# Attention of a decoder trunk: the last rotation two steps behind the last projection, and the last head's output normed and split by halves

## The chip, the cores and the metric

The kernel runs on one core of a Trainium2 chip. The metric is the device time of one launch in microseconds (us), as the median of three runs. Five engines work beside each other: TensorE (PE, with its weight loads PEld), VectorE (DVE), ScalarE (ACT), GpSimd (POOL) and SyncE (SP), which only issues DMAs here.

## The reference, cut to what matters

Two layers over 1024 positions of width 1024, in float32: gated linear attention with its MLP, then differential attention with its MLP. The change lies in the second layer's attention:

```python
k, v = shared_kv(h, kv_norm_w, w_kv, cos, sin)     # projections, rotary on k
q = apply_rope((a_in @ w_q), cos, sin)             # 8 heads, two q and two k of width 64 each
p = softmax(where(causal, q @ k.T * scale, -inf))  # per head and pair
a = p[:, 0] - lam * p[:, 1]                        # the differential weights
o = rmsnorm(a @ v, subln_w) * (1 - lam_init)       # per head, width 128
h = h + o.reshape(S, 1024) @ w_o
```

Rotary is x * cos + rot(x) * sin, where rot swaps the two halves of a head and negates one.

## The kernel before

Every float32 product is made of three products of a rounded high part and a rest: hi x hi, hi x lo, lo x hi (names ending in h and l: xh and xl, wh and wl, ah and al). The high part is an ACT copy, the low part a DVE or POOL subtraction (helper `lo_of`, line 115, or `tt`, line 112).

The attention is one loop over steps s = -2, -1, ... for 8 heads of 8 query blocks (64 blocks in all). Step s issues, in this order: the scores of block s+2 (sp); the values of a pair of blocks if s-1 is odd (pv: the weighted sum of v, then ACT copies osq and osb out of it); `turn(s)` (PE transposes the weights e into tp, ACT copies them to ah, DVE makes al); `combine(s+1)` (DVE makes e from two exponentials); `weights(s+2)` (DVE takes the row maximum mx, ACT the exponential e); splits of the next head's q, k and v; then the step's fill units; and the norm of the head that ended: `squares` and `norm1` at s-2 (DVE rs_m, POOL's power rs_y), `norm2` at s-3 (DVE rs_t, ro) and `finish` at s-4 (PE spreads ro over rows into rb, DVE multiplies osb by it).

Fill units keep PE busy between these. `spread(units, s0, s1)` spreads a list evenly over steps s0 to s1. There are 48 projection half-units (`rope_unit`, twelve matmuls into pf each) for the q and k of heads 2 to 7. Four make one q or k: the second part of each half ends in an ACT copy xsb and a DVE product y with the cosines; after the second half SP issues four DMAs that put xsb's halves in swapped places (xw). At the start of the next unit `rope_end` lets POOL multiply xw by the sines and add it to y, and a later unit stores y to DRAM (kd, qd), from where it is loaded as st and split. Only the last rotation is called on its own, on DVE (RE). A weight tile is fetched with `take`: ACT makes wh, DVE wl, and DVE multiplies the next raw tile by the norm's gains.

The outputs of heads 0 to 5 are stored (osp) and loaded again (osr, `o_load`), then split by an ACT copy xh and eight POOL subtractions for two tiles (`o_split`). Sixteen units of the output projection (`wo_unit`, into dwo) for heads 0 to 3 fill the last steps; those of heads 4 to 7 follow the loop, and six of them begin inside it with three of their four parts (heads 4 to 6), so that only the last head is missing.

PE, ACT and SP go in written order (`manual_schedule`); the order of DVE and POOL is set by a scheduler at build time. PSUM has two double-bank tiles for scores and output products and four single banks for all else (pf, tp, pv, rb, sv).

Of the kernel before, what the change touches and what calls it, by code (L numbers as in the profile page):

```python
# [10 lines left out]
F32R = mybir.dt.float32r  # L11
BF16 = mybir.dt.bfloat16
AF = mybir.ActivationFunctionType
ALU = mybir.AluOpType
# [6 lines left out]
NB = S // P  # L21
# [4 lines left out]
AH, HD, VD = 8, 64, 128  # L26
# [4 lines left out]
DORD = (0, 4, 1, 5, 2, 6, 3, 7)  # L31
# [17 lines left out]
def trunk(  # L49
# [26 lines left out]
    PE, ACT, DVE, POOL = nc.tensor, nc.scalar, nc.vector, nc.gpsimd  # L76
# [10 lines left out]
    def uid(s):  # L87
        count[0] += 1
        return f"{s}_{count[0]}"

    def U(name, dt=F32):
        return up.tile([P, 1026], dt, tag="u", name=uid(name))[:, 0:1024]
# [4 lines left out]
    def PS(name):  # L97
        return pp.tile([P, 512], F32, tag="p", name=uid(name))

    def PS2(name):  # L100
        return pp.tile([P, 1024], F32, tag="p2", name=uid(name), bufs=2)
# [6 lines left out]
    def H(hf):  # L108
        return slice(hf * HALF, (hf + 1) * HALF)

    def tt(eng, o, a, b, op):
        eng.tensor_tensor(out=o, in0=a, in1=b, op=op)  # L112

    def stt(eng, o, a, s, b, op0, op1):
        eng.scalar_tensor_tensor(out=o, in0=a, scalar=s, in1=b, op0=op0, op1=op1)  # L115

    def lo_of(eng, lo, x, hi, scale=1.0):
        stt(eng, lo, x, scale, hi.bitcast(F32), ALU.mult, ALU.subtract)
# [144 lines left out]
    def take():  # L263
        prefetch(1)
        r = ready.popleft()
        prefetch(AHEAD)
        return r
# [37 lines left out]
    def bcast_rows(col8, sl):  # L305

        ps = PS("rb")
        for i, b in enumerate(range(sl.start // P, sl.stop // P)):
            PE.matmul(ps[:, i * P:(i + 1) * P], col8[:, b:b + 1].broadcast_to([P, P]), ident, start=True, stop=True)  # L309
        return ps  # L310

    def fine(eng, o, a, b, op):

        for c in range(0, 1024, 256 if eng is POOL else 1024):
            q = slice(c, c + 256 if eng is POOL else 1024)
            tt(eng, o[:, q], a[:, q], b[:, q], op)

    def split(x, scale=1.0, eng=DVE):
        xh = U("xh", F32R)
        xl = U("xl", F32R)  # L320
        ACT.activation(xh, x, AF.Copy, scale=scale)
        if eng is POOL:
            fine(POOL, xl, x, xh.bitcast(F32), ALU.subtract)
        else:
            lo_of(DVE, xl, x, xh, scale)
        return xh, xl
# [92 lines left out]
    class Late:  # L419
# [44 lines left out]
        def spread(self, sl):  # L464
            ps = bcast_rows(self.rtok, sl)[:, 0:sl.stop - sl.start]
            if self.g is None:
                DVE.tensor_copy(self.rbc[:, sl], ps)
                return
            ACT.activation(self.rbc[:, sl], ps, AF.Copy)
            for q in range(0, sl.stop - sl.start, 256):  # L470
                self.ps[sl.start + q] = ps[:, q:q + 256]
# [713 lines left out]
    sub_w = const.tile([P, 1], F32, name="sub_w")  # L1185
# [85 lines left out]
    def kq_units(hh):  # L1271
        return [(rope_unit, dst, sc, hf, part) for dst, sc in ((kd[hh], 1.0), (qd[hh], HD ** -0.5))
                for hf in range(2) for part in range(2)]

    class Attn:
# [130 lines left out]
        def finish(self):  # L1406
            for hf in range(2):
                stt(DVE, self.osb[:, H(hf)], self.osb[:, H(hf)], sub_w, bcast_rows(self.ro, H(hf)), ALU.mult, ALU.mult)

    osp = [dram.tile([P, S], F32, name=f"osp{i}") for i in range(AH - 2)]  # L1410
    h, on, wdo = {}, [], {}
    n1 = Wide(G_FFN1, hs[1])
# [15 lines left out]
    def o_split():  # L1428
        on.append(split(osr.popleft(), eng=OE))

    def wo_unit(g, d, hf, ks=range(4)):

        e, j = divmod(d, 4)
        if (g, j) not in wdo:
            wdo[g, j] = take() + ([None] * 4,)
            if g == 1 and j < 2:
                t = PS2("dwo")
                wdo[g, j][2][0], wdo[g, j][2][2] = t[:, H(0)], t[:, H(1)]
        wh, wl, ops = wdo[g, j]
        u = e * 2 + hf  # L1440
        if ops[u] is None:
            ops[u] = PS("dwo")
        o = ops[u]
        sl = H(hf)
        for k in ks:
            wd = slice(k * 2 * P + e * P, k * 2 * P + e * P + P)
            a, b = on[4 * g + k]
            PE.matmul(o, wh[:, wd], a[:, sl], start=(k == 0), stop=False)  # L1448
            PE.matmul(o, wl[:, wd], a[:, sl], start=False, stop=False)  # L1449
            PE.matmul(o, wh[:, wd], b[:, sl], start=False, stop=(k == 3))  # L1450
        if 3 not in ks:
            return
        ops[u] = None
        tt(DVE, h[d][:, sl], o, h[d][:, sl], ALU.add)
        if g == 1:
            n1.add(d, hf, h[d])
        if hf == 1:
            if e == 1:
                del wdo[g, j]
            if d == ND - 1:  # L1460
                on[4 * g:4 * g + 4] = [None] * 4

    steps = AH * NB
    OE = POOL
    KQE, OL, OS, RS, WOB, RE = 46, 45, 46, 47, 48, DVE
    AHEAD, LOADS = 1, 2
    heads = {0: Attn(0)}
    todo = {0: [(heads[0].load, 2)], 6: [(heads[0].load, 1)], 9: [(heads[0].qk_split, 1), (heads[0].v_split,)],
# [9 lines left out]
    fill = {s: [] for s in range(-2, steps)}  # L1478
# [4 lines left out]
            fill[s0 + s] += units[len(units) * s // n:len(units) * (s + 1) // n]  # L1483

    spread([u for a in range(2, AH) for u in kq_units(a)], -2, KQE)
    fill[KQE + 1].append((rope_end, RE))
    fill[KQE + 1].append((rope_end,))
    spread([(o_load, q) for q in range(4)], OL, OL + 1)
    spread([(o_split,) for q in range(4)], OS, OS + 1)
    fill[RS] += [(residual, d) for d in DORD]  # L1490
    spread([(o_load, q) for q in (4, 5)], steps - 4, steps - 3)
    spread([(wo_unit, 0, d, hf) for d in DORD for hf in range(2)], WOB, steps - 1)

    for s in range(-2, steps + 5):
        a, i = divmod(s + 2, NB)
        if a < AH:
            hd = heads[a]
            if i == 0:
                hd.begin()
            hd.scores(i)  # L1500
        b, j = divmod(s - 1, NB)
        if 0 <= s - 1 < steps and j % 2 == 1:
            heads[b].values(j // 2)
        b, j = divmod(s, NB)
        if 0 <= s < steps:
            heads[b].turn(j)
        if 0 <= s + 1 < steps:
            b, j = divmod(s + 1, NB)
            heads[b].combine(j)
            if j % 2 == 0:  # L1510
                heads[b].clear(j // 2)
        if a < AH:
            hd.weights(i)
            if i == 1 and a > 0:
                hd.v_split()
            if a + 1 < AH:
                if i == 2:
                    heads[a + 1] = Attn(a + 1)
                    heads[a + 1].load(1)
                if i == 4:  # L1520
                    heads[a + 1].load(0)
                    heads[a + 1].qk_split(1)
                if i == 6:
                    heads[a + 1].qk_split(0)
                    heads[a + 1].load(2)
        for f, *args in fill.pop(s, ()):
            f(*args)
        if 0 <= s - 2 < steps:
            b, j = divmod(s - 2, NB)
            if j % 2 == 1:  # L1530
                heads[b].squares(j // 2)
            if j == NB - 1:
                heads[b].norm1()
        if 0 <= s - 3 < steps:
            b, j = divmod(s - 3, NB)
            if j == NB - 1:
                heads[b].norm2()
        if 0 <= s - 4 < steps:
            b, j = divmod(s - 4, NB)
            if j == NB - 1:  # L1540
                hd = heads.pop(b)
                hd.finish()
                if b < AH - 2:
                    nc.sync.dma_start(osp[b], hd.osb)
                elif b == AH - 2:
                    last = [split(hd.osb, eng=POOL)]
                else:
                    last.append(split(hd.osb))
        if s == steps - 1:
            AHEAD, LOADS, WENG = 1, 3, DVE  # L1550
            o_split()
            o_split()
            on.append(last[0])
        if steps <= s < steps + 3:
            for d in DORD[2 * (s - steps):2 * (s - steps) + 2]:
                wo_unit(1, d, 0, range(3))
    on.append(last[1])
    for hf in range(2):
        for u, d in enumerate(DORD):
# [110 lines left out]
```

## Time and profile before

| | before |
|---|---|
| median of three runs | 2395.2 us (2393.8 to 2397.9) |
| profiled execution | 2395.9 us, of which the span 2393.9 us |
| PE busy | 2320.7 us, 97% of the span |
| DVE, ACT, POOL busy | 77%, 43%, 30% |
| attention loop | about 1251 to 1667 us |

The profile follows one execution; busy time is that of instructions, and the idle time of an engine is put down to what released it. [...]

### The profile page before, as it was taken

What the parts mean: (1) busy time and instruction counts of PE and PEld (TensorE: products, weight loads), DVE (VectorE), ACT (ScalarE), POOL (GpSimd) and SP (SyncE); (2) the same over time, 40 slices, a digit from 0 to 9 for tenths busy, and PEclk for the clock granted to TensorE, in tenths of its full rate; (3) what the DMA queues carried; (4) which work ended last, traced back from release to release, by engine and by line L of the source; (5) the groups of instructions that cost most, each with busy time, mean ns of one, the idle gap of its engine ahead of it and who ended that gap; (6) DMA issues with size and microseconds to landing.
All of it is one profiled execution on the core that took longest, in us unless ns stands there. A gap on an engine that the chain in (4) does not pass through costs nothing. (4 is left out here: it accounts for less than half of the span.)

```text
span 2393.9 us, 29738 instructions
## 1 busy us (share of the span) xinstructions
PE 2320.7 (97%) x10926; PEld 1878.5 (78%) x10926; DVE 1832.5 (77%) x2599; ACT 1040.5 (43%) x1864; POOL 729.8 (30%) x725
## 2 busy tenths in 40 slices
PE   8999999999999999999999999999999999999998
PEld 6878877767888888888877888777767888888886
DVE  7454454699999999867138787666799999999875
ACT  4533442354333434544125555544344443334553
POOL 3211101045544431000005564623036554441001
PEclk9999999999999999999999999999899999999999
DMA  5012124113323248424243333522213333238433
GB/s 184 1 53 71 36 98 171 61 52 116 115 84 115 84 165 304 133 85 171 79 128 118 113 123 93 163 107 84 84 35 117 113 100 115 84 126 317 142 92 101
DMA packets 101425, 271.22 MB, mean 113 GB/s; under 512 B 10272, under 2 KB 23200, under 8 KB 101280
## 3 DMA queue, kind: packets, MB, share of 16 engines
q1 hardware_dynamic: 101280, 269.34, 32.8%
q8 instruction: 85, 1.39, 0.2%
q14 instruction: 60, 0.49, 0.1%
HBM read 184.89 MB, written 76.02 MB: 109 GB/s over the span
## 5 line engine op out<-in xcount | busy, mean ns | idle before, releaser
L899 PE MATMUL pf<-xp,wp 128*128 128x512 f32 x1232 | 488.5, 397 | 12.8 <-DVE wp L115 12.7
L900 PE MATMUL pf<-xp,wp 128*128 128x512 f32 x1232 | 488.0, 396 | 1.8 <-DVE xp L115 1.4
L898 PE MATMUL pf<-xp,wp 128*128 128x512 f32 x1232 | 487.8, 396 | 1.5 <-ACT xp L206 1.2
L899 PEld LDWEIGHTS pf<-xp,wp 128*128 128x128 f32 x1232 | 232.2, 188 | 73.4 <-DVE wp L115 19.5
L898 PEld LDWEIGHTS pf<-xp,wp 128*128 128x128 f32 x1232 | 232.2, 189 | 58.9 <-ACT xp L206 3.2
L900 PEld LDWEIGHTS pf<-xp,wp 128*128 128x128 f32 x1232 | 232.0, 188 | 58.8 <-DVE xp L115 5.4
L1007 PE MATMUL out<-rp,lp 128*128 128x512 f32 (+1 forms) x632 | 246.4, 390 | 0.6 <-ACT rp L206 0.6
L1009 PE MATMUL out<-rp,lp 128*128 128x512 f32 (+1 forms) x632 | 246.1, 389 | 0.0
L115 DVE SCALAR_TENSOR_TENSOR c<-u,cv,c 128x1024 f32<-128x1024 f32 x176 | 245.9, 1399 | 0.0
L1008 PE MATMUL out<-rp,lp 128*128 128x512 f32 (+1 forms) x632 | 245.5, 388 | 0.0
L115 DVE SCALAR_TENSOR_TENSOR wp<-raw,wp 128x512 fp32r<-128x512 f32 x180 | 202.5, 1134 | 13.2 <-ACT wp L206 12.9
L112 DVE TENSOR_TENSOR u<-pf,u 128x512 f32<-128x512 f32 x300 | 200.6, 681 | 15.0 <-PE pf L900 10.0
L276 PE MATMUL pf<-xh,wh 128*128 128x512 f32 x458 | 187.4, 409 | 8.9 <-ACT wh L196 8.9
L277 PE MATMUL pf<-xh,wl 128*128 128x512 f32 x458 | 181.6, 396 | 1.8 <-DVE wl L115 1.8
L278 PE MATMUL pf<-xl,wh 128*128 128x512 f32 x458 | 181.1, 395 | 0.0
L112 POOL TENSOR_TENSOR rs_y<-rs_m,nhalf 128x4 f32<-128x4 f32 (+2 forms) x26 | 31.4, 1206 | 481.8 <-DVE rs_m L292 451.1
L925 ACT ACTIVATE c<-c 128x1024 f32<-128x1024 f32 x44 | 46.7, 1062 | 267.0 <-DVE c L115 267.0
L115 DVE SCALAR_TENSOR_TENSOR wp<-wt,wp 128x512 fp32r<-128x512 f32 x128 | 151.6, 1186 | 2.5 <-ACT wp L206 2.5
L1007 PEld LDWEIGHTS out<-rp,lp 128*128 128x128 f32 x632 | 118.7, 188 | 27.5 <-ACT rp L206 1.1
L1009 PEld LDWEIGHTS out<-rp,lp 128*128 128x128 f32 x632 | 118.7, 188 | 27.6 <-DVE rp L115 0.8
L1008 PEld LDWEIGHTS out<-rp,lp 128*128 128x128 f32 x632 | 118.8, 188 | 26.8
L112 POOL TENSOR_TENSOR wt<-raw,wt 128x512 f32<-128x512 f32 x40 | 56.9, 1423 | 253.9 <-DVE wp L115 253.9
(250 smaller groups left out, 4997.8 us busy)
## 6 DMA issues: line engine op xcount, KB each, us to landing
raw<-in_w_in SPq DMA_DIRECT2D x88, 512.0 KB, 3.8
tr<-td SPq DMA_DIRECT2D x70, 512.0 KB, 4.0
td<-c SPq DMA_DIRECT2D x44, 512.0 KB, 2.8
wo<-in_w_out SPq DMA_DIRECT2D x44, 512.0 KB, 8.4
raw<-in_w_gla SPq DMA_DIRECT2D x24, 512.0 KB, 5.9
h<-hs SPq DMA_DIRECT2D x24, 512.0 KB, 4.9
td<-mt SPq DMA_DIRECT2D x22, 512.0 KB, 3.8
hs<-h SPq DMA_DIRECT2D x32, 256.0 KB, 2.0
```

The source lines that it names most:

```text
L112: eng.tensor_tensor(out=o, in0=a, in1=b, op=op)
L115: eng.scalar_tensor_tensor(out=o, in0=a, scalar=s, in1=b, op0=op0, op1=op1)
L276: PE.matmul(o, wh[:, k], xh[:, H(hf)], start=(k == 0), stop=False)
L277: PE.matmul(o, wl[:, k], xh[:, H(hf)], start=False, stop=False)
L278: PE.matmul(o, wh[:, k], xl[:, H(hf)], start=False, stop=(k == ND - 1))
L898: PE.matmul(o, wh, xh, start=(k == 0), stop=False)
L899: PE.matmul(o, wl, xh, start=False, stop=False)
L900: PE.matmul(o, wh, xl, start=False, stop=(k == ND // 2 - 1))
L925: ACT.activation(gt, gt, AF.Silu)
L1007: PE.matmul(o, wh, xh, start=(j == 0 or cut and j == NJ - LASTF), stop=False)
L1008: PE.matmul(o, wl, xh, start=False, stop=False)
L1009: PE.matmul(o, wh, xl, start=False, stop=(j == NJ - 1 or cut and j == NJ - LASTF - 1))
```

## The change

Six constants and the end of the loop are changed. KQE, the last step with a projection unit, goes from 46 to 45, so each unit of all heads comes one step sooner, the first at step -2. The last rotation stays at step 47 and its store moves to step 48. The loads of the first four heads' outputs go from steps 45 and 46 to 44 and 45 (OL), their splits from 46 and 47 to 44 and 45, into the same step as the load (OS). The residual loads go from step 47 to 46 (RS). The output units' first step goes from 48 to 47 (WOB); 16 units over 17 steps leave the first of them empty, so they stay where they are. For the last head, `finish` and the split of a whole tile, which came after all six three-part output products, become `finish_split` between the fifth and the sixth, half by half.

```diff
+        def finish_split(self):
+            xh, xl = U("xh", F32R), U("xl", F32R)
+            for hf in range(2):
+                o = self.osb[:, H(hf)]
+                stt(DVE, o, o, sub_w, bcast_rows(self.ro, H(hf)), ALU.mult, ALU.mult)
+                ACT.activation(xh[:, H(hf)], o, AF.Copy)
+                lo_of(DVE, xl[:, H(hf)], o, xh[:, H(hf)])
+            return xh, xl
...
-    KQE, OL, OS, RS, WOB, RE = 46, 45, 46, 47, 48, DVE
+    KQE, OL, OS, RS, WOB, RE = 45, 44, 44, 46, 47, DVE
...
-    fill[KQE + 1].append((rope_end, RE))
-    fill[KQE + 1].append((rope_end,))
+    fill[KQE + 2].append((rope_end, RE))
+    fill[KQE + 3].append((rope_end,))
...
-    for s in range(-2, steps + 5):
+    for s in range(-2, steps + 3):
...
-            if j == NB - 1:
+            if j == NB - 1 and b < AH - 1:
...
-                elif b == AH - 2:
+                else:
                     last = [split(hd.osb, eng=POOL)]
-                else:
-                    last.append(split(hd.osb))
...
-            for d in DORD[2 * (s - steps):2 * (s - steps) + 2]:
-                wo_unit(1, d, 0, range(3))
+            for u in range(2 * (s - steps), 2 * (s - steps) + 2):
+                if u == 5:
+                    last.append(heads.pop(AH - 1).finish_split())
+                wo_unit(1, DORD[u], 0, range(3))
```

The scheduler's order on DVE follows. First DVE in a regular head, from the 768-wide maxima (mx) or just behind them to the 896-wide ones; wl is a weight tile's low part and raw the next tile times the gains. Before:

```order
L115 SCALAR_TENSOR_TENSOR e_12011<-e_12012,rc_12107,e_12011 128x768
L115 SCALAR_TENSOR_TENSOR wl_12026<-raw_11763,wh_12025 128x1024
L115 SCALAR_TENSOR_TENSOR osb_11058<-osb_11058,sub_w,rb_12051 128x512
L115 SCALAR_TENSOR_TENSOR osb_11058<-osb_11058,sub_w,rb_12057 128x512
L1340 TENSOR_REDUCE mx_12111<-sp_12064 128x1
L1340 TENSOR_REDUCE mx_12111<-sp_12065 128x1
L112 TENSOR_TENSOR raw_12030<-raw_12030,gains_sb 128x1024
```

And now:

```order
L115 SCALAR_TENSOR_TENSOR wl_11981<-raw_11720,wh_11980 128x1024
L1340 TENSOR_REDUCE mx_12040<-sp_12007 128x1
L115 SCALAR_TENSOR_TENSOR al_11883<-tp_12023,ah_11882 128x4x128
L1340 TENSOR_REDUCE mx_12040<-sp_12008 128x1
L1396 COPY ss_11651<-sv_12062 128x2
L112 TENSOR_TENSOR raw_11985<-raw_11985,gains_sb 128x1024
L115 SCALAR_TENSOR_TENSOR y_11988<-pf_11989,cosr_9172 128x512
L115 SCALAR_TENSOR_TENSOR osb_11077<-osb_11077,sub_w,rb_12066 128x512
L115 SCALAR_TENSOR_TENSOR osb_11077<-osb_11077,sub_w,rb_12072 128x512
```

The weight's wl stands ahead of the 768-wide maxima, and raw and a y stand ahead of the 896-wide ones, which follow after the products osb and the 768-wide e.

Then ACT in steps 45 to 47, around the copies xh<-osr. Before, from xsb of the last unit:

```order
L1261 ACTIVATE xsb_12604<-pf_12759 128x512
L321 ACTIVATE xh_12860<-osr_12772 128x1024
L321 ACTIVATE xh_12867<-osr_12774 128x1024
L1373 ACTIVATE ah_12746<-tp_12883 128x4x128
L1373 ACTIVATE ah_12747<-tp_12890 128x4x128
L1341 ACTIVATE e_12906,s_2178_12782<-sp_12874,mx_12905 128x256
L1341 ACTIVATE e_12906,s_2179_12783<-sp_12874,mx_12905 128x256
L321 ACTIVATE xh_12910<-st_12697 128x1024
L321 ACTIVATE xh_12920<-osr_12856 128x1024
```

And now:

```order
L1341 ACTIVATE e_12785,s_2067_12226<-sp_12745,mx_12783 128x1024
L1261 ACTIVATE xsb_12559<-pf_12714 128x512
L321 ACTIVATE xh_12813<-osr_12809 128x1024
L321 ACTIVATE xh_12820<-osr_12811 128x1024
L1387 ACTIVATE osq_12863<-pv_12844 128x256
L1388 ACTIVATE osb_12223<-pv_12844 128x256
L1373 ACTIVATE ah_12777<-tp_12866 128x4x128
L1373 ACTIVATE ah_12778<-tp_12873 128x3x128
```

The third and fourth of these copies stood behind ah and the exponentials of step 47; they now stand right behind xsb, ahead of osq, osb and ah of step 46.

Last DVE at step 50, around the norm of head 5 (rs_m, rs_t, ro) and the al of block 49. Before:

```order
L1396 COPY ss_12205<-sv_13067 128x2
L115 SCALAR_TENSOR_TENSOR rs_m_13073<-ss_12205,s_2065_12206 128x8
L112 TENSOR_TENSOR rs_t_13143<-rs_m_13073,rs_y_13074 128x8
L112 TENSOR_TENSOR rs_t_13143<-rs_t_13143,rs_y_13074 128x8
L302 TENSOR_SCALAR rs_t_13143<-rs_t_13143 128x8
L112 TENSOR_TENSOR ro_13071<-rs_y_13074,rs_t_13143 128x8
L1348 RECIPROCAL rc_13040<-s_2179_12783 128x1
L115 SCALAR_TENSOR_TENSOR rc_13040<-s_2178_12782,nlam,rc_13040 128x1
L115 SCALAR_TENSOR_TENSOR e_13000<-e_13000,rc_13040 128x384
L115 SCALAR_TENSOR_TENSOR wl_13007<-raw_12602,wh_13006 128x1024
L115 SCALAR_TENSOR_TENSOR al_12902<-tp_13035,ah_12901 128x2x128
```

And now:

```order
L115 SCALAR_TENSOR_TENSOR e_12999<-e_12999,rc_13040 128x384
L1335 TENSOR_REDUCE mx_13048<-sp_13026 128x2
L115 SCALAR_TENSOR_TENSOR wl_13007<-raw_12557,wh_13006 128x1024
L115 SCALAR_TENSOR_TENSOR al_12932<-tp_13035,ah_12931 128x2x128
L112 TENSOR_TENSOR h_12888<-dwo_13053,h_12888 128x512
L1396 COPY ss_12224<-sv_13067 128x2
L1348 RECIPROCAL rc_13109<-s_2190_12834 128x1
L115 SCALAR_TENSOR_TENSOR rs_m_13073<-ss_12224,s_2066_12225 128x8
L115 SCALAR_TENSOR_TENSOR rc_13109<-s_2189_12833,nlam,rc_13109 128x1
L112 TENSOR_TENSOR rs_t_13143<-rs_m_13073,rs_y_13074 128x8
```

The al of block 49 stood behind the norm chain and now stands ahead of it.

## Rows read from the trace of the kernel before

**Rows 1.** The page, part 1: busy us, share of the span, instructions

```profile
PE 2320.7 (97%) x10926; PEld 1878.5 (78%) x10926; DVE 1832.5 (77%) x2599; ACT 1040.5 (43%) x1864; POOL 729.8 (30%) x725
```

**Rows 2.** Waits of PE, 1250 to 1720: us in total, times, longest

```profile
PE pv L1385 <- DVE al L115: 8.9, 2, 5.0
PE sp L1323 <- ACT e L1341: 4.5, 8, 1.7
...
PE dwo L1448 <- DVE h L112: 1.6, 2, 0.8
PE tp L1369 <- DVE e L115: 1.2, 1, 1.2
PE dwo L1450 <- POOL xl L112: 1.1, 1, 1.1
```

**Rows 3.** Stretches: us, PE, PEld, DVE, ACT, POOL busy, granted clock, DMA share, GB/s

```profile
1262.00:1275.00 13.00, 11.30 (x58) 8.61 (x57) 9.57 (x17) 6.50 (x18) 6.89 (x8) 0.87 0.38 138
...
1541.00:1558.00 17.00, 10.74 (x66) 9.01 (x65) 8.07 (x12) 10.33 (x20) 15.15 (x21) 0.80 0.78 265
1558.00:1574.00 16.00, 12.05 (x61) 9.60 (x62) 10.14 (x23) 5.46 (x13) 3.64 (x6) 0.79 0.52 213
...
1667.00:1690.00 23.00, 18.91 (x71) 14.20 (x70) 13.23 (x19) 6.62 (x10) 4.11 (x4) 0.78 0.23 87
```

**Rows 4.** Timeline in a head, DVE, ACT, PE: start, us, instruction, idle before, releaser

```profile
1516.96 0.69 DVE L115 SCALAR_TENSOR_TENSOR y<-pf,cosr 128x512 f32<-128x512 f32 x1
...
1520.45 0.16 DVE L1348 RECIPROCAL rc<-s 128x1 f32<-128x1 f32 x1 [0.48 <-ACT e L1341]
...
1527.84 1.04 ACT L1341 ACTIVATE e<-sp,mx 128x896 f32<-128x896 f32 x1
...
1528.90 0.62 PE L1323 MATMUL sp<-xh,xh 64*128 64x512 f32 x2
```

**Rows 5.** Groups by line and form, DVE, 1300 to 1541: busy us, mean ns

```profile
L112 DVE TENSOR_TENSOR raw<-raw,gains_sb 128x1024 f32<-128x1024 f32 x8 | 10.9, 1368 | 0.0
```

**Rows 6.** Timeline around the first al wait: PE, ACT, SP

```profile
1535.45 0.19 ACT L1341 ACTIVATION_READ_ACCUMULATOR e<-sp,mx 128x1 f32 x1
...
1538.17 0.48 PE L276 MATMUL pf<-xh,wh 128*128 128x512 f32 x1
...
1541.23 0.60 ACT L1261 ACTIVATE xsb<-pf 128x512 f32<-128x512 f32 x1 [1.32 <-PE pf L278]
...
1541.85 2.42 SPq L1268 DMA_DIRECT2D xw<-xsb  x4
1544.37 1.02 SPq L1425 DMA_DIRECT2D osr<-osp  x2
...
1547.83 1.06 ACT L321 ACTIVATE xh<-osr 128x1024 fp32r<-128x1024 f32 x1 [1.28 <-DMA osr<-osp]
1549.62 1.06 ACT L321 ACTIVATE xh<-osr 128x1024 fp32r<-128x1024 f32 x1 [0.73 <-DMA osr<-osp]
...
1549.74 0.58 PE L1385 MATMUL pv<-al,xh 128*128 128x256 f32 x1 [4.98 <-DVE al L115]
```

**Rows 7.** Timeline around the second al wait: DVE, PE

```profile
1565.21 0.17 DVE L112 TENSOR_TENSOR rs_t<-rs_m,rs_y 128x8 f32<-128x8 f32 x1 [1.76 <-POOL rs_y L112]
...
1568.49 0.58 PE L1385 MATMUL pv<-al,xh 128*128 128x256 f32 x1 [3.95 <-DVE al L115]
```

**Rows 8.** Timeline at the end of the last head: PE, DVE, ACT

```profile
1667.43 1.95 PE L309 MATMUL rb<-ident,ro 128*128 128x128 f32 x16
...
1668.52 1.64 DVE L115 SCALAR_TENSOR_TENSOR osb<-osb,sub_w,rb 128x512 f32<-128x512 f32 x2 [4.83 <-PE rb L309]
...
1670.26 1.06 ACT L321 ACTIVATE xh<-osb 128x1024 fp32r<-128x1024 f32 x1 [12.07 <-DVE osb L115]
...
1671.35 1.23 DVE L115 SCALAR_TENSOR_TENSOR xl<-osb,xh 128x1024 fp32r<-128x1024 f32 x1 [1.18 <-ACT xh L321]
...
1671.37 0.50 PE L1448 MATMUL dwo<-xh,wh 128*128 128x512 f32 x1 [1.99 <-ACT xh L321]
```

## The prediction, made before the changed kernel was run

> **What bounds the kernel now.** I read the page first, then the waits of TensorE (PE), then stretches, then single instructions. PE is busy 97% of the span [rows 1], so a reordering can win only what PE spends idle or at the lower of its two clock levels. Between 1250 and 1720 us, where the change lies, the waits are few [rows 2]: two of a value product (pv) for the DVE's low parts al, 8.9 us together; eight of the scores for an exponential, 4.5; one of a transpose for a weight tile, 1.2; one of an output product for a GpSimd split, 1.1. [...]
>
> The profiled execution took 2395.9 us, 0.7 above the median of 2395.2. I sum against it and take 0.7 off at the end.
>
> **The change part by part.** Instruction counts are equal but for the last head's two splits, which become four halves. Everything else is order.
>
> *Start.* The 48 projection units come one step sooner; the first is now at step -2. One unit lasts about 3.0 us (from 1538.17 to just before the copy at 1541.23 [rows 6]). At step -2 PE had nothing between the scores of blocks 0 and 1, while DVE prepared weights: the 1.2 wait and the longest exponential wait of 1.7 follow from that [rows 2]. Three us more PE work ahead of both cover 2.9 less what DVE still owes; its queue holds the same items with one wide multiplication now ahead of a maximum, and I leave 0.6 idle: 2.3 gained. The clock gives more: 0.13 of 13 us twice is 3.4 us at the low level, of which 1.7 idle, so 0.85 to 1.7 saved; I take 1.3. Start: -3.6 (bounds -1.0, DVE as late as before, and -4.6).
>
> *Heads 0 to 5.* What a unit triggers moves from even to odd steps. In each head DVE now does y (0.69) ahead of the norm chain and of the 640-wide maxima, and in heads 0 to 4 also raw times gains ahead of the 896-wide maxima, where it stood behind them. This chain had no slack: the last 896-wide exponential ended at 1527.84 + 1.04 = 1528.88 and PE began the next scores, which need its bank, at 1528.90 [rows 4]. The multiplication takes 1.37 on average [rows 5]. Of the 0.69 + 1.37 = 2.06 a head, part falls into gaps where DVE waited for an exponential anyway (0.48 ahead of one of them [rows 4]). If all of it hides the cost is nothing; if none does, 5 x 2.06 = 10.3. Nearest is the middle: the y delays the 640-wide maxima fully (0.6), the multiplication leaves about 0.3. Five heads: +4.5 (0 to +10.3; below nothing is excluded since nothing of DVE's was removed).
>
> *The last rotation and the first al wait.* Before, DVE waited for the rotated copy's DMA, multiplied and added, and only then made al; PE waited 4.98 [rows 6]. Now the last unit is at step 45, so the copy, its four DMAs and the rotation are ahead of both block 46 and 47. But the split of each earlier head's output now stands in the step of its load: ACT's copies xh<-osr 2 and 3 sit right behind the copy xsb, ahead of osq, osb and ah of blocks 46 and 47. On SyncE their loads stand behind the four xw issues. I count in the old times and add the moved unit after. The exponentials of step 45 ended at 1535.64; xsb adds 0.60: 1536.2; the xw issues 2.42: 1538.7. The two copies began 3.46 and 5.25 after their loads' issue began at 1544.37 [rows 6], so now at 1542.2 and 1543.9; the second ends at 1545.0. Behind it on ACT wait osq and osb, and for the bank that osb frees PE's second transpose tile of block 47; then ah, an exponential pair and ah again: some five pieces of up to 512 columns at the 0.60 of xsb, then DVE's al, about the same, so pv goes on near 1548.7. Steps -2 to 45 hold one unit more, so that is 1551.7, against 1549.74. PE, which has no unit left in steps 46 and 47, stands some 6 us in place of 5. Cost +2.0, and 0.7 for a longer low clock: +2.7. Bounds: loads landing at once, -5 and its clock of about 1.4; loads slowed by the eight residual loads issued behind them, +6.
>
> [...]
>
> *The second al wait.* DVE stood 1.76 for GpSimd's power [rows 7], and behind that in its queue were a weight tile, a split of a weight and the al that PE waited 3.95 for. In the new DVE order that al is ahead of the norm chain: the 3.95 goes. What is late next is the weight tile of block 49, now queued behind the first output addition: about 0.7 (one 512-wide addition). Low clock: 0.21 of 16 us twice is 6.7, less the idle 3.95, so 1.4 to 3.4 saved; I take 2.0. Together -3.95 - 2.0 + 0.7 = -5.3 (-7 to -1). The 1.1 wait for GpSimd's split goes too, since those splits begin some 5 us sooner against the output product: -1.1.
>
> *The end of the last head.* The row broadcast (rb, 1.95) leaves the end of six three-part products for a place before the sixth, whose nine matmuls (about 2.2 us, three quarters of a projection unit's twelve) now follow it. Before: rb from 1667.43, DVE's two products 1.64, ACT 1.06, DVE 1.23, and PE idle 1.99 [rows 8]. With halves the first half needs one product (0.8), one ACT copy (0.6, as xsb) and one DVE split (0.7, half of 1.23 and a start); the first product can start after half of rb, so the first half is complete some 2 us after rb ends, behind the sixth unit. In the stretch PE idled 23 - 18.91 = 4.1 [rows 3], of which 1.6 behind the additions h of a shared bank [rows 2] stays: 2.5 idle gone. Low clock: 0.22 of 23 twice is 10.1, less 4.1 idle, so 3.0 to 5.0 saved if the clock never falls; I take 3.3. End: -5.8 (-7.5 to -3).
>
> The output units at steps 48 to 63 (WOB) do not move: 16 units over 17 steps leave the first step empty. Nothing.
>
> Sum: -3.6 + 4.5 + 2.7 - 5.3 - 1.1 - 5.8 = -8.6, so 2395.9 - 8.6 - 0.7 = 2386.6.
>
> **The rivals.**
> *All stalls go.* The osr loads land before ACT reaches them and the heads hide their moved work: first al wait -5 in place of +2.7, heads +1 in place of +4.5: near 2376; half of that, 2380, is more like it. For: ACT is 43% busy. Against: the SyncE order puts osr behind the xw issues.
> *ACT held by the copies.* The loads share the DMA engines with eight residual loads behind them and land 4 us later still; with the low clock that is +6.4: 2393. For: in this stretch the DMA share was 0.78 [rows 3]. Against: the loads are issued first.
> *The heads pay in full (slower).* DVE gets the whole 2.06 late in heads 0 to 4, and each idle of that length drops the clock as the 1.7 one at the start did, 1.3 more: 5 x 3.4 = 17 in place of 4.5: 2399. It decides from a cost of 2.6 us a head, where the 13.1 of the other terms is eaten. For: no slack in rows 4. Against: DVE's gaps there.
> *The halves buy nothing.* DVE takes both products before a half split and ACT starts late; PE waits as long, one unit sooner: 2392.
>
> **How the numbers follow.** Forecast 0.42; all stalls go 0.17; held ACT 0.24; heads in full 0.13; halves 0.04. A measurement of this kernel can tell about 0.2%, 4.8 us. Faster (under 2390.4): nearly all of the forecast's, 0.17, and 0.04 of held ACT: 0.60. Slower (over 2400.0): most of the heads' case: 0.10. The rest 0.30. The range leaves out the better half of the first rival and most of the third: 2378 to 2396.
>
> **What would show it.** Right: no wait of pv for al near the second place; no wait of dwo for ACT's xh at the end and a clock near 1.00 there; a wait of some 6 us in step 47 ended by ACT (osb or ah) behind xh<-osr; scores waiting 0.3 to 1 for an exponential twice a head. Wrong: the first stall unchanged with the DVE rotation as its releaser; clock below 1.00 inside heads 1 to 4; a 2-us idle left behind rb.

## The result and the profile after

The changed kernel takes 2420.78 us (median of four, 2419.09 to 2424.35), the kernel before 2395.48 (four, 2393.82 to 2397.9). The ratio is 1.0102, with a 95% interval of 1.009 to 1.0114: slower by about 25 us. 2386.6 had been predicted, faster by 9; the range ended at 2396.

The page first: how long each engine was busy. PE was busy 16.5 us longer than in [rows 1] with the same 10926 matmuls.

```profile
PE 2337.2 (97%) x10926; PEld 1889.3 (78%) x10926; DVE 1841.5 (76%) x2600; ACT 1040.3 (43%) x1865; POOL 728.8 (30%) x725
```

The waits of PE, 1250 to 1750 us (total, times, longest), answer to [rows 2]:

```profile
PE sp L1323 <- ACT e L1341: 23.0, 26, 3.4
PE tp L1369 <- ACT osb L1388: 6.1, 1, 6.1
PE st L386 <- DVE ssq L112: 4.2, 1, 4.2
PE dwo L1458 <- DVE h L112: 2.1, 2, 1.4
```

Both waits of pv for al (8.9 together) are gone, as is the one for GpSimd's xl, and the clock of the start and of the end recovered. But the scores wait 26 times and 23.0 us for an exponential, where they waited 8 times and 4.5. The 4.2 of st is in the kernel before too (4.18), at the norm behind the attention.

The stretches (length, busy time of PE, PEld, DVE, ACT and POOL, granted clock of PE as a share of full speed, DMA share, GB/s), to be read against [rows 3]: the start, a stretch inside heads 1 to 4, the stretch from about step 44 on, and two of the end.

```profile
1250.00:1270.00 20.00, 18.37 (x93) 12.64 (x91) 14.20 (x22) 7.41 (x21) 4.96 (x8) 1.00 0.44 135
...
1333.00:1532.00 199.00, 185.27 (x1132) 151.50 (x1131) 148.09 (x248) 97.56 (x221) 105.39 (x141) 0.93 0.31 94
1558.00:1610.00 52.00, 42.35 (x251) 33.88 (x250) 32.74 (x63) 27.93 (x61) 24.82 (x39) 0.90 0.57 203
1610.00:1690.00 80.00, 79.45 (x518) 67.30 (x518) 57.56 (x106) 40.15 (x85) 19.10 (x31) 1.00 0.21 69
1690.00:1720.00 30.00, 27.86 (x132) 22.47 (x131) 18.59 (x30) 8.05 (x13) 10.90 (x8) 1.00 0.35 130
```

The same stretch of time in the kernel before, which there gets through a little more than four heads: PE 197.52 of 199 us, clock 1.00.

```profile
1333.00:1532.00 199.00, 197.52 (x1289) 163.81 (x1288) 153.59 (x280) 112.37 (x256) 113.50 (x155) 1.00 0.37 115
```

A ledger from the starts of the same PE instructions in both traces, before and after: to the second wait of the start 17.1 and 18.3 us, a unit of 3.0 having moved in, so -1.8 like for like; from there to the first regular place of head 1 54.3 and 59.2, +4.9; four head periods 192.6 and 218.4, +25.8; from there to step 55 78.7 and 76.5, the same unit having gone, so +0.8; to the norm behind the attention 124.8 and 118.7, -6.1. With 0.8 ahead and 1.0 behind, and the unit cancelling, the sum is 25.4; the spans differ by 25.5. **The loss is in the regular heads**, 6.45 us in each, and 4.9 more in head 0.

What happens there is seen in one head: POOL, SP, DVE, ACT and PE in order of start (start, us, instruction; in brackets idle time before it and its releaser).

```profile
1502.68 3.54 POOL L112 TENSOR_TENSOR y<-y,xw 128x256 f32<-128x256 f32 x4
1505.56 2.07 DVE L1340 TENSOR_REDUCE mx<-sp 128x1 f32<-128x896 f32 x2
1506.26 0.32 SPq L1244 DMA_DIRECT2D kd<-y  x1
1508.96 1.01 ACT L1341 ACTIVATE e<-sp,mx 128x896 f32<-128x896 f32 x1 [3.64 <-DMA kd<-y]
...
1510.11 0.79 PE L1323 MATMUL sp<-xh,xh 64*128 64x512 f32 x1 [2.81 <-ACT e L1341]
...
1511.10 0.79 PE L1323 MATMUL sp<-xh,xh 64*128 64x512 f32 x1 [0.20 <-ACT e L1341]
```

The first of the two 896-wide maxima was ready near 1506.6 (half of 2.07 after 1505.56). The exponential did not begin then: it waited until 1508.96 **for a store to DRAM of a rotated k that it has nothing to do with**. The link is a buffer. Work tiles come from one pool of 44 equal slots (called U in the code), given out in the order in which the program asks; the exponential's result e got the slot of y. The slot is free only when y's store has landed, the store waits for POOL's rotation, and the shift of the units put that rotation into the very stretch in which e is written. In the built program six exponentials wait for such a store, against one before; in the trace five of them stand for it, one in each of heads 1 to 5. ACT's waits, 1250 to 1560, after:

```profile
ACT e L1341 <- DVE mx L1340: 26.2, 23, 2.1
ACT e L1341 <- DMA kd<-y: 14.5, 4, 3.6
```

and before, where the second kind is missing:

```profile
ACT e L1341 <- DVE mx L1340: 17.0, 22, 2.0
```

So in each of heads 1 to 4 ACT waits 3.6, of which 2.4 lie behind the ready maximum, PE stands 2.81 + 0.20 there and 0.28 + 0.28 at the narrower place (3.6 in all), and the clock falls: 0.93 over these heads. In each of these heads PE has some 6.8 us in a row at a granted clock of 0.50 (read by single microseconds; in head 1 from 1346.2 to 1353.0), which by that number is worth 3.4 us at 1.00 (an estimate). Of the 6.45 us a head some 3.3 are idle time beyond that of before, and the rest goes with the low clock.

Head 0 loses by another link of the same kind. SyncE's DMAs stand in written order here. Before, it issued the load of head 1's k (st<-kd) at 1261.07, ahead of a store of a rotated q (qd<-y) at 1269.74. With the units a step sooner the store stands first, and it waits for POOL's rotation, which ended at 1271.31. After (SP, then ACT):

```profile
1271.34 0.33 SPq L1244 DMA_DIRECT2D qd<-y  x1
1271.76 1.40 SPq L1289 DMA_DIRECT2D st<-kd  x1
```

```profile
1279.29 1.06 ACT L321 ACTIVATE xh<-st 128x1024 fp32r<-128x1024 f32 x1 [2.99 <-DMA st<-kd]
```

ACT's copy xh stands 2.99 us for that load, where it did not wait before. Behind it on ACT comes the weight's wh; DVE waits 3.46 for wh to make wl; and behind wl follow the 768-wide maximum, its exponential and PE, which stands 3.42. The copy waits for that load in the traces of all seven kernels with the sooner units, and in none of the seven with the units at their old steps (experiments below). The cost went with the load: in e4 it landed 7.6 us after its issue and PE stood 3.83 and 0.67, in e11 4.8 us and 1.08 and 0.97. No run put the load back ahead of the store.

### The profile page after: what moved, and what is told of

The parts are those of the page before. It is cut to its first block, busy times and chain, and to the rows that moved or that the text cites. A ratio compares the mean times of both kernels' runs of the same rounds, so it can differ in the third digit from the quotient of the medians.

```text
span 2419.4 us, 29730 instructions
## 1 busy us (share of the span) xinstructions
PE 2337.2 (97%) x10926; PEld 1889.3 (78%) x10926; DVE 1841.5 (76%) x2600; ACT 1040.3 (43%) x1865; POOL 728.8 (30%) x725
## 5 line engine op out<-in xcount | busy, mean ns | idle before, releaser
L1009 PEld LDWEIGHTS out<-rp,lp 128*128 128x128 f32 x632 | 118.7, 188 | 27.3 <-DVE rp L115 0.8
L1007 PEld LDWEIGHTS out<-rp,lp 128*128 128x128 f32 x632 | 118.7, 188 | 27.0 <-ACT rp L206 0.6
```

What stands on the lines that cost most here:

```text
L1007: PE.matmul(o, wh, xh, start=(j == 0 or cut and j == NJ - LASTF), stop=False)
L1009: PE.matmul(o, wh, xl, start=False, stop=(j == NJ - 1 or cut and j == NJ - LASTF - 1))
```

## The experiments

Each ratio is against the kernel before on the same chip, with its 95% interval; all diffs but the first are against the changed kernel.

**e1: the shift of the units alone** (against the kernel before; the last rotation stays at step 47).

```diff
-    KQE, OL, OS, RS, WOB, RE = 46, 45, 46, 47, 48, DVE
+    KQE, OL, OS, RS, WOB, RE = 45, 45, 46, 47, 48, DVE
...
-    fill[KQE + 1].append((rope_end, RE))
-    fill[KQE + 1].append((rope_end,))
+    fill[47].append((rope_end, RE))
+    fill[48].append((rope_end,))
```

> Kernel before with only the projection units a step sooner (last unit at step 45, last rotation at 47, its store at 48); loads and splits of the earlier heads' outputs, residual loads and the end of the last head as before. Theory 1 (the shift of the units is the whole loss: in heads 1 to 4 the exponential of the 896-wide block gets the buffer that y had and waits for y's store to DRAM): 2420 to 2430 us, scores waiting 2.5 to 3 us for that exponential once a head, released by the store kd<-y. Rival (the loss needs the new places of the osr copies): within 5 us of 2395.

Measured: 2430.0 (2427.86 to 2433.42), ratio 1.0134 [1.012, 1.0148]. The time is at the upper end of Theory 1. Its wait of the scores is that of the whole change, and so is ACT's for the store (PE 1250 to 1750, ACT 1250 to 1560):

```profile
PE sp L1323 <- ACT e L1341: 23.4, 25, 3.8
```

```profile
ACT e L1341 <- DMA kd<-y: 14.6, 4, 3.7
```

The shift alone costs more than the whole change loses; the other parts give some of it back.

**e2: the halves of the last head alone** (steps as before, `finish_split` kept).

```diff
-    KQE, OL, OS, RS, WOB, RE = 45, 44, 44, 46, 47, DVE
+    KQE, OL, OS, RS, WOB, RE = 46, 45, 46, 47, 48, DVE
...
-    fill[KQE + 2].append((rope_end, RE))
-    fill[KQE + 3].append((rope_end,))
+    fill[KQE + 1].append((rope_end, RE))
+    fill[KQE + 1].append((rope_end,))
```

> Kernel before with only the last head's output normed and split by halves ahead of the sixth unit. Theory: the end gains what the changed kernel's end shows, 2388 to 2391 us (5 to 7 us faster), no wait of the output product for ACT's xh, clock near 1.00 between 1660 and 1690. Rival (the halves only help when the loop before them has changed): within 2 us of 2395.

Measured: 2389.66, ratio 0.9968 [0.9957, 0.998], a gain of about 8 us (5 to 10). The ledger of the whole change showed 6.1 for the same place.

**e3: everything but the shift** (units, rotation and store at their old steps; early loads and splits, halves).

```diff
-    KQE, OL, OS, RS, WOB, RE = 45, 44, 44, 46, 47, DVE
+    KQE, OL, OS, RS, WOB, RE = 46, 44, 44, 46, 47, DVE
...
-    fill[KQE + 2].append((rope_end, RE))
-    fill[KQE + 3].append((rope_end,))
+    fill[KQE + 1].append((rope_end, RE))
+    fill[KQE + 1].append((rope_end,))
```

> Changed kernel with the projection units at their old steps (last one at 46, rotation and store at 47); loads, splits and residual loads a step or two sooner, and the halves at the end, as in the changed kernel. Theory: the heads are as before, so 2387 to 2394 us; the first wait for al stays (5 us or more, since the last unit is at step 46 again and ACT copies osr beside it), the end is short. Rival (the sooner osr loads cost as much as the units): over 2405.

Measured: 2388.16, ratio 0.9959 [0.9947, 0.9972]. Both al waits are gone here too, without the shift; the theory had the first one stay. In their place the scores wait once, behind an ACT that waits for loads (PE, then ACT):

```profile
1543.08 0.58 PE L1323 MATMUL sp<-xh,xh 64*128 64x256 f32 x2 [4.92 <-ACT e L1341]
```

```profile
1537.77 1.06 ACT L321 ACTIVATE xh<-osr 128x1024 fp32r<-128x1024 f32 x1 [3.88 <-DMA osr<-osp]
1540.12 1.06 ACT L321 ACTIVATE xh<-osr 128x1024 fp32r<-128x1024 f32 x1 [1.29 <-DMA osr<-osp]
```

**e4: y in two buffers of its own** (the common pool is two slots smaller to make room).

```diff
-NSLOT = 44
+NSLOT = 42
...
-            rp["y"] = U("y")
+            rp["y"] = up.tile([P, 1024], F32, tag="y", name=uid("y"), bufs=2)
```

> Changed kernel with y (the product with the cosines) in two buffers of its own and two fewer in the common ring, so that no exponential can get y's buffer and wait for its store to DRAM. Theory 1 (that wait is the larger part of the loss in heads 1 to 4): the wait of the 896-wide exponential for kd<-y is gone, the idle ahead of the scores falls from 2.8 to under 1 us a head, the clock in heads 1 to 4 is 1.00, time 2398 to 2408 us. Theory 2 (the DVE order is the loss: the weight's wl and raw times gains ahead of the maxima): the exponential waits for its maximum until nearly as late, time 2414 to 2421.

Measured: 2409.62 (2408.42 to 2411.13), ratio 1.0047 [1.003, 1.0064]; against 1.0102 that is 0.55%, 13 us back. The time is 1.6 above the range of Theory 1. Its other signs came: no exponential waits for a store of y any more, 1.0 of idle time is left at that place, and in heads 1 to 4 the clock is whole again:

```profile
1333.00:1532.00 199.00, 192.94 (x1249) 158.17 (x1248) 157.07 (x274) 107.42 (x246) 111.29 (x148) 1.00 0.36 107
```

A head period is 49.7 us, against 54.6 in the change and 48.15 before: the buffer with its low clock is 4.9 a head, and 1.5 are left, idle time of 0.5 at each of two places. Four heads at 4.9 are 20 us, more than the 13 that came back. The smaller pool also deals the other slots differently, outside the attention too, where the change alters nothing. The starts of PE's first score product and of the norm behind the attention, and the end of the span, in us of one trace each:

| | first scores | norm | end | attention | behind it |
|---|---|---|---|---|---|
| before | 1251.56 | 1718.98 | 2393.9 | 467.4 | 674.9 |
| change | 1252.39 | 1743.52 | 2419.4 | 491.1 | 675.9 |
| e4 | 1255.60 | 1729.40 | 2408.4 | 473.8 | 679.0 |
| e9 | 1257.20 | 1723.55 | 2400.8 | 466.4 | 677.3 |
| e11 | 1259.33 | 1717.92 | 2397.1 | 458.6 | 679.2 |

In the attention e4 gives back 17.3. Ahead of it the eleven traces with 44 slots took 1251.6 to 1255.0, the three with 42 slots (and y in its own buffers) 1255.6 to 1259.3. So the smaller pool seems to cost some microseconds there. That is not shown: no run had it alone.

**e5: without the product of the weights with the gains in the loop.** This kernel leaves out the multiplication of the second layer's projection weights by the norm's gains inside the attention loop.

```diff
+    skipg = False
...
-            tt(eng, rv, rv, gb, ALU.mult)
+            if not (skipg and gi in (G_KV, G_ATTN1) and nk == 8):
+                tt(eng, rv, rv, gb, ALU.mult)
...
+    skipg = True
```

> Changed kernel that leaves out the multiplication of the raw q and k weights by the norm's gains inside the attention loop (so q and k of heads 2 to 7 miss that factor); the buffers fall differently and no exponential of the heads waits for a store of y any more. Theory 1: 2394 to 2404, close to the kernel with y in its own buffers, some 2 to 5 us below it, since 1.7 us of DVE work ahead of the maxima is gone too. Theory 2 (raw ahead of the maxima is the loss): 10 us or more below the kernel with y in its own buffers.

Measured: 2412.96 (2407.4 to 2414.16), ratio 1.0057 [1.0042, 1.0072]. The expectation rested on a mistake: the buffer wait is still in this kernel, five times.

```profile
ACT e L1343 <- DMA kd<-y: 13.2, 5, 2.6
```

So the run does not price the multiplication by itself; that needed e9. It showed something else, under the last heading.

**e6: units at their old steps, but the last two both at step 45**, so that the last rotation is early without the shift.

```diff
-    spread([u for a in range(2, AH) for u in kq_units(a)], -2, KQE)
+    units = [u for a in range(2, AH) for u in kq_units(a)]
+    spread(units[:-1], -1, KQE)
+    fill[KQE].append(units[-1])
```

> Changed kernel with all projection units at their old steps but the last, which comes with the last but one at step 45; rotation at 47, store at 48. Theory: heads as before, the end short, the last rotation ahead of the al of blocks 46 and 47 as in the changed kernel, but ACT still held by the osr copies: 2384 to 2392 us. Rival (ACT held by the copies costs what the rotation saved, and PE without a unit in step 46 stands longer): 2392 to 2398.

Measured: 2389.38, ratio 0.9965 [0.9951, 0.9978]. The heads are free of the loss, but PE waits 4.07 for osb at 1549.83: ACT is held by the copies of osr as in the whole change. The time is in the range of the theory, which had foreseen this, and no better than e3.

**e7, e8, e10: the loads of osr at steps 42 and 43**, so that the copies find their data: on e3, on e6 and on the change itself. The edit is one number.

```diff
-    KQE, OL, OS, RS, WOB, RE = 45, 44, 44, 46, 47, DVE
+    KQE, OL, OS, RS, WOB, RE = 45, 42, 44, 46, 47, DVE
```

> The kernel with the units at their old steps (sooner loads and splits, halves at the end) with the loads of the four earlier outputs two steps sooner still (steps 42 and 43), so that each split copy finds its tile landed. Theory (ACT is held by copies that wait for their load): the wait of 4.9 us for an exponential near 1543 goes and its low clock with it, 2381 to 2385 us. Rival (the copies are not what holds ACT, or DVE and PE wait for something else at the same place): 2386 to 2390.

> The kernel with the last unit doubled into step 45, with the loads two steps sooner (42 and 43). Theory: the wait of 4.1 us for ACT's osb goes, 2381 to 2386 us, about level with the kernel that keeps the old units. Rival: PE, with no unit in step 46, waits for DVE's rotation or al instead: 2387 to 2391.

> Changed kernel with the loads of the earlier outputs at steps 42 and 43 and nothing else altered. Theory: the 6.1 us wait of the transposes for ACT's osb, behind the copies that wait for their load, falls to 2 us or less, 5 to 9 us below the changed kernel (2412 to 2416); the heads stay as slow. Rival (the wait is ACT's own work, not the load): within 3 us of the changed kernel.

Measured: e7 2387.48, ratio 0.9957 [0.9944, 0.9971]; e8 2391.04, 0.997 [0.9959, 0.998]; e10 2411.23, 1.006 [1.0047, 1.0073]. The theories of e7 and e8 failed: both times are those of their rivals. The gain of e10 is a little above its theory's.

On the change itself the loads are worth 0.42%, 10 us. The 6.1 of PE for osb is gone, and so is the low clock of this stretch (it was 0.93 over 1532 to 1610):

```profile
1532.00:1610.00 78.00, 74.14 (x491) 60.71 (x489) 60.30 (x113) 42.91 (x98) 43.17 (x62) 1.00 0.52 176
```

On e3 and e6 they are worth nothing, since another wait stands in the same place. In e7 the 4.92 becomes 2.41 of the scores and 2.42 of a transpose; in e8 one longer wait of a transpose, behind two DVE instructions (DVE, then PE, then POOL, in e8):

```profile
1543.97 2.97 DVE L115 SCALAR_TENSOR_TENSOR rc<-s,nlam,rc 128x1 f32<-128x1 f32 x1
1546.98 6.76 DVE L115 SCALAR_TENSOR_TENSOR e<-e,rc,e 128x1024 f32<-128x1024 f32 x1
```

```profile
1554.40 1.97 PE L1369 MATMUL tp<-ident,e 128*128 128x128 f32 x8 [7.16 <-DVE y L115]
```

```profile
1541.32 5.61 POOL L112 TENSOR_TENSOR xl<-osr,xh 128x256 fp32r<-128x256 f32 x8
...
1547.17 5.49 POOL L112 TENSOR_TENSOR xl<-osr,xh 128x256 fp32r<-128x256 f32 x8
```

The combination e lasts 6.76 us, where this shape takes 1.29 in the kernel before: with the early loads POOL's sixteen subtractions of osr follow each other with only two short memsets between them and lie over it (last heading).

**e9: own buffers for y, and no product with the gains** (e4 and e5 together; the same multiplication is left out).

> Changed kernel with y in two buffers of its own and without the multiplication of the raw q and k weights by the gains inside the attention loop (that factor is missing in q and k of heads 2 to 7). Theory (buffer wait and DVE order are the whole loss in the heads, and add up): idle ahead of the scores in heads 1 to 4 under 0.5 us a head, a head's period within 0.5 us of the 48.2 of before, time 2397 to 2404, most of what is left over 2392 in head 0 and in step 45. Rival (the shift costs something else in the heads): a period of 49 us or more.

Measured: 2404.03 (2401.61 to 2404.92), ratio 1.0024 [1.0014, 1.0034]. A head period is 48.7. So of the 1.5 that e4 left, the multiplication ahead of the maxima is 1.0; the other 0.5 is put down to the rest of the DVE's order, which no run changed. PE still waits 3.09 and 0.67 in head 0, 5.96 of the scores and 3.98 of a transpose behind the copies of osr. Even so its attention part takes 466.4 us, 1.1 less than before (table at e4): in this trace what is left above 1 lies ahead of the attention and behind it.

**e11: both causes taken away** (own buffers for y as in e4, loads at 42 as in e10).

> Changed kernel with both waits' causes taken away: y in two buffers of its own (ring two smaller), and the loads of the earlier outputs at steps 42 and 43. Theory (the two are separate and add up): 13 us from y's buffer and 10 from the sooner loads below the changed kernel, 2396 to 2402 us, a head's period in heads 1 to 4 still 1.4 us over that of the kernel before, since DVE's order stays. Rival (one of them hides the other): 2404 or more.

Measured: 2399.15 (2392.88 to 2402.47), ratio 1.0008 [0.9999, 1.0017]. The two causes add up: 0.55% and 0.42% apart, 0.94% together. In its trace the attention part is 8.8 us shorter than in the kernel before (table at e4); the stretch ahead of it is 7.8 longer, the one behind it 4.3. The longest wait of the scores is 1.1:

```profile
PE sp L1323 <- ACT e L1341: 10.9, 25, 1.1
```

**e12: units at their old steps, halves, loads at 44 and 45, and the splits a step behind them** (residual loads at 47).

```diff
-    KQE, OL, OS, RS, WOB, RE = 45, 44, 44, 46, 47, DVE
+    KQE, OL, OS, RS, WOB, RE = 46, 44, 45, 47, 48, DVE
...
-    fill[KQE + 2].append((rope_end, RE))
-    fill[KQE + 3].append((rope_end,))
+    fill[KQE + 1].append((rope_end, RE))
+    fill[KQE + 1].append((rope_end,))
```

> Units at their old steps, halves at the end, loads at steps 44 and 45, splits a step after the load (45 and 46); residual loads (47) and first output unit (48) as in the kernel before. Theory (ACT copies that come a step after their load do not wait, and the second al wait is gone with the scheduler's new order): 2383 to 2388 us. Rival (the al waits of the kernel before come back): 2388 to 2391, as with the halves alone.

Measured: 2387.29 (2379.69 to 2388.38), ratio 0.9953 [0.9941, 0.9966]. The time is in the theory's range, but the theory was half wrong: the first al wait shrinks from 4.98 [rows 6] to 1.01, and the second is back at 4.87, against 3.95 [rows 7], as its rival had it:

```profile
PE pv L1385 <- DVE al L115: 5.9, 2, 4.9
```

With e3 and e7 it is the best version found, 0.4 to 0.5% faster than the kernel before; their intervals overlap that of the halves alone (e2), so that the halves are shown and the rest of the gain is not told apart.

## Why the prediction was wrong, step by step

**The heads (+4.5, bounds 0 to +10.3): the step that failed.** It costed what a moved unit adds to DVE's queue, y and the multiplication, and nothing else. But a unit also triggers POOL's rotation and the store, and these moved into the stretch of the 896-wide exponentials. The step put them at nothing and gave no reason. What tied them to the chain was not data but the slot of a buffer, which the views of before can't show; the waits in the built program did show it. The upper end was a bound for DVE only. Measured: +25.8 in four periods, and +4.9 ahead of them in head 0 (PE waits 3.42 and 0.67 after against 0.89 before), where a moved store delays a load on SyncE. The DVE's part alone, which the step did cost, was 0.9 a head and measured 1.5 (e4), of which 1.0 is the multiplication (e9), where 0.3 had been taken: it hid less, at 1.70 an instruction after against 1.37 in [rows 5].

**The rival of heads that pay in full (2399).** It had the place and the sign, even the fall of the clock, with another mechanism: 3.4 a head by DVE's order. With that order alone (e4) the cost was 1.5 and the clock was 1.00. Had the time come out at 2399, it would have been luck. (The sum of the rival in which all stalls go is 2375.4, and half of it 2381.0, where the text has 2376 and 2380; nothing hangs on that.)

**The first al wait (+2.7): right in mechanism.** It said that ACT would be held by the copies xh<-osr ahead of osq and osb and PE would stand some 6 us in place of 5. ACT, then PE, after:

```profile
1580.17 1.06 ACT L321 ACTIVATE xh<-osr 128x1024 fp32r<-128x1024 f32 x1 [6.60 <-DMA osr<-osp]
1581.40 1.06 ACT L321 ACTIVATE xh<-osr 128x1024 fp32r<-128x1024 f32 x1 [0.17 <-DMA osr<-osp]
1582.36 0.37 ACT L1387 ACTIVATE osq<-pv 128x256 f32<-128x256 f32 x1
1582.63 0.38 ACT L1388 ACTIVATE osb<-pv 128x256 f32<-128x256 f32 x1
```

```profile
1583.06 1.12 PE L1369 MATMUL tp<-ident,e 128*128 128x128 f32 x4 [6.06 <-ACT osb L1388]
```

PE stands 6.06, released by osb behind the two copies. ACT is idle for 6.60 ahead of the first: SyncE issues the four of xw from 1573.60 on, 2.41 long, and the two loads behind them at 1576.05, and the copy begins 4.12 later. The prediction's count had osq, osb and the ah behind the two copies, as ACT's written order has them, and so they ran: the product that osq and osb copy began its last matmul at 1574.74, and the two began at 1582.36 and 1582.63, the two ah at 1582.89. Loads two steps earlier, with all else in place, give 10 us (e10): the idle 6 is gone, and the clock over 1532 to 1610 is 1.00 in place of 0.93.

**The second al wait (-5.3) and GpSimd's split (-1.1).** Both waits are gone, as predicted, and of the predicted 0.7 behind the first output addition 0.52 came: the transposes of block 49 stand for its e, which follows that addition on DVE (DVE, then PE, after).

```profile
1594.60 0.48 DVE L115 SCALAR_TENSOR_TENSOR e<-e,rc 128x256 f32<-128x256 f32 x1
```

```profile
1595.14 0.44 PE L1369 MATMUL tp<-ident,e 128*128 128x128 f32 x2 [0.52 <-DVE e L115]
```

Their gain can't be read alone: the stretch from the last regular place to step 55 came out at +0.8, with 6.06 of the copies, 2.3 of head 5 (1.82 and 0.49) and the clock of 0.90 in it.

**The start (-3.6): right in mechanism, its size half seen.** PE waits 0.35 and 0.69 in place of 1.2 and 1.7 [rows 2], and the clock is 1.00 and 0.99 (1250 to 1270 and 1270 to 1285) in place of 0.87 [rows 3]; -1.8 was gained up to the second wait. The low-clock terms of the prediction take twice what a stretch's clock is short of 1.00 as time at the low level. In the trace of before single microseconds bear that out: 1.00 up to 1269, 0.50 from 1270 to 1273, 1.00 again from 1274. What the clock gave behind it can't be read, since it lies in the row of the ledger in which head 0 lost.

**The end (-5.8): right, -6.1 measured.** The row broadcast is followed by matmuls that cover it, and ACT needs 0.64 for the first half, where 0.6 had been taken. The wait of 1.99 of [rows 8] is gone, the clock is 1.00 where it was 0.78, and the wait for h stays, 2.1 us, as predicted (1.6). The end of the last head after:

```profile
1696.07 1.95 PE L309 MATMUL rb<-ident,ro 128*128 128x128 f32 x16
1697.16 1.64 DVE L115 SCALAR_TENSOR_TENSOR osb<-osb,sub_w,rb 128x512 f32<-128x512 f32 x2 [2.75 <-PE rb L309]
...
1697.77 0.48 PE L1458 MATMUL dwo<-xh,wh 128*128 128x512 f32 x1
...
1697.94 0.64 ACT L1416 ACTIVATE xh<-osb 128x512 fp32r<-128x512 f32 x1 [9.06 <-DVE osb L115]
```

Without the buffer and without the held ACT (e11) the kernel is still no faster than before: 2399.15, 1.0008. But its attention part is 8.8 us shorter in the trace, with the DVE's 1.5 in each regular head still in it; what it gains there is lost outside (table at e4).

**What stays open.** Three things were not tried: the load of head 1's k put back ahead of the store, the pool of 42 slots alone, and the shift with another order on DVE. So whether the shift would pay without the wait for the buffer and without a smaller pool is not known. The kernel with the units at their old steps (e3) has 454.5 us in the attention part of its trace, less than e11.

## What to carry to other kernels

A moved step takes its stores and the life of its buffers with it: where tiles come from a common ring, list for each moved store which later write takes its slot, and put the landing of the store, not the last use of its data, into the sum. What is "off the critical path" by its data can be on it by its buffer. Here 3.3 us more idle time in a head went with 6.8 us at a granted clock of 0.50, and the head took 6.45 us longer, four times over. The same goes for an issuing queue in written order: here a store that waited for POOL (qd<-y, issued at 1271.34) held the load written behind it (st<-kd, at 1271.76, where it was at 1261.07 before). And a buffer taken out of a ring makes the ring smaller for all others, so read the stages that weren't touched as well. A change of one step everywhere for the sake of one wait at the end was the wrong size: e3 removed both of those waits, and e12 most of the first, without touching the regular heads.

## What the runs showed of the hardware

**At the same idle time the granted clock fell in some heads and not in others.** In e5 PE stands 1.8 us, and 0.3 to 0.5 just behind, in each of heads 1 to 4 at the same place. The periods of these four heads are 52.6, 53.7, 52.5 and 51.0 us, and their stretches have granted clocks of 0.97, 0.94, 0.97 and 1.00; the second and the fourth (columns as above):

```profile
1382.00:1436.00 54.00, 51.23 (x313) 41.82 (x313) 36.82 (x67) 27.08 (x63) 26.09 (x37) 0.94 0.33 99
...
1488.00:1539.00 51.00, 48.12 (x313) 39.59 (x312) 35.94 (x68) 26.83 (x62) 26.06 (x37) 1.00 0.35 104
```

In the change, with 2.81 + 0.20 there, the clock was 0.94 in each of the four periods; in e4, with 0.5 at each of two places, it was 1.00. So in e5's trace heads with the same idle time differ by up to 2.7 us.

**DVE's times beside POOL's subtractions.** In e8 the DVE's rc, 128 numbers, takes 2.97 us (0.26 on average in the kernel before) and ends at 1546.94, when POOL's first eight subtractions end (1546.93). The e behind it takes 6.76 and ends 1.1 us after POOL's second eight. In e7 it is the same: e from 1547.52, 6.85 long, ends 1.09 after POOL's second eight, which run from 1547.72 for 5.56.

So in these two traces DVE's e ended only behind all eight of POOL's second subtractions. It isn't always so: in e10 the same e took 1.73, from 1575.79, inside POOL's first eight (from 1572.22, 6.60 long), and in the kernel before POOL's first eight took 7.50 beside DVE's work (5.60 the next eight), while DVE's xw and y there took 1.27 and 1.63. That POOL's rotation beside it is what makes raw times gains 1.70 us in the changed kernel against 1.35 before (averages over 1320 to 1541) is argued from the order of time only; no run had the one without the other.
